# Products of 256 columns that stream their operand in exchanged runs of 16, in place of a shifted operand, in a two-layer diffusion transformer on one core

## The chip, the core and the metric

The kernel runs on one core of a Trainium2 chip. A core has a matrix engine (PE; its weight loads are listed apart, as PEld), a vector engine (DVE), a scalar engine (ACT), GpSimd (POOL), and SyncE (SP), which here only issues transfers. Matrix products read both operands from SBUF and accumulate in PSUM, which has eight banks of 512 float32 columns in each of 128 partitions. The metric is the device time of one execution in microseconds. The kernel before took 1179.38 us, the median of three runs (1178.57 to 1179.57).

A product on PE has two operands. The stationary one, `lhsT`, at most 128 columns, is put into the array by a weight load. The streamed one, `rhs`, here mostly 256 or 512 columns, then runs through the array, and each streamed column gives one column of output in PSUM. In the profile, each product is one LDWEIGHTS on PEld and one MATMUL on PE.

## The reference

One batch of 256 latent tokens and 256 context tokens, model width 1024, two layers. Layer 0 mixes by retention (4 heads, two directions) and treats both kinds of tokens; layer 1 mixes by neighbourhood attention (32 heads) and gives the latent tokens alone. After each mixer comes a gated residual, a layer norm, and an MLP of width 4096 with a squared relu:

```python
def sq_relu_mlp(h, w1, w2):
    return jnp.square(jax.nn.relu(h @ w1)) @ w2

def reference(x, c, ctx, ...):
    for i in range(DEPTH):
        ...
        x = layer_norm(DN_ALPHA * x + g1 * y, ln_g[i, 0], ln_b[i, 0])
        h = x * (1.0 + sc2) + sh2
        x = layer_norm(DN_ALPHA * x + g2 * sq_relu_mlp(h, mlp_w1[i], mlp_w2[i]), ln_g[i, 1], ln_b[i, 1])
        ...
    return x
```

All arrays are float32. The first layer's MLP is called the first MLP below, the second layer's the second MLP.

## The kernel before

**Three products for one.** Every float32 operand of a large product is split into a high part (rounded, by a cast on ACT) and a low part (the rest, by a subtraction on DVE), both of type float32r. The helper `mm3` (line 174) issues high·high, high·low and low·high into one accumulating output. In names, `hi` and `lo` are the parts of a weight, `hTh` and `hTl` those of the modulated tokens (model columns on the partitions; 8 blocks of 512 token columns, the 256 latent tokens first), `hid` those of an MLP's hidden layer, `oTh` and `oTl` those of the attention's output.

**Where 256 columns are streamed.** Most products stream 512 columns. Those with 256 are, in order of the program:

- `masked_scores` (line 1062): the retention's scores for the keys of the latent tokens, output `pS`;
- `mm1` with the latent columns and `ctx_mm1` with the context columns, for the first two blocks of the first MLP (lines 1254 and 1263), output `p1`;
- `q_mm` and part of `k_mm` (line 1445 on), the attention's queries and keys of the latent tokens, output `pn`;
- `mmo` (line 1694) with half a bank, in the attention's output projection, output `pnw`;
- `tok_part` (line 1975), the first block of the second MLP, in which the tokens are the stationary operand and the weights are streamed, output `p1t`;
- `mm1` for the other 14 blocks of the second MLP's first product, weights stationary and tokens streamed, output `p1`;
- `mm2b` (line 2094) for the last 512 columns of the second tile's output in the second MLP, which are computed in two halves of 256, output `p2`.

The profile leaves trailing digits off names, so that `p1` and `p2` are both `p` there; they are told apart by the operands (`hT…` or `hid`).

**The shift.** Every large tile starts at the same place modulo 1024 bytes, and a slice of a weight or of the tokens starts at a multiple of 128 float32 (512 bytes) from its tile's start. So the start of the streamed operand and that of the next product's stationary operand differ by a multiple of 512 bytes. The second MLP is the exception. There the token tiles' columns begin at `AT = 7 * LINE` with `LINE = 16` float32 (64 bytes): its modulated tokens are written to columns 112 to 367 of each block instead of 0 to 255, and read from there. All else in that MLP (weights, hidden layer) is unshifted. This is line 1933 with the helper `toks` in line 1937; `mm1` is told by its argument `at=AT`.

**What sets the order.** PE runs its products in the program's order. Weights come in units of 512 KB: SP fetches a unit into one of four raw tiles, ACT makes the high part and DVE the low part, into one of five buffers each. In the stretches around the change PE's own instructions are all that the program has to do in order, with `relu_sq`, the splits of weights, and norms on ACT and DVE beside it.

Of the kernel before, what the change touches and what calls it, by code (L numbers as in the profile page):

```python
# [17 lines left out]
P = 128  # L18
# [18 lines left out]
LINE = 16  # L37
# [67 lines left out]
def kernel(  # L105
# [23 lines left out]
    pe, act, dve, pool, sp = (  # L129
        InOrder(tc, getattr(nc, e), e in PIN)  # L130
        for e in ("tensor", "scalar", "vector", "gpsimd", "sync")
    )
# [23 lines left out]
    def bank(s="ps"):  # L156
        return psp.tile([P, 512], F32, tag="ps", name=nm(s))

    def slot(i, shape, dt, s):

        return arena.tile(shape, dt, tag=f"s{i}", name=nm(s))
# [4 lines left out]
    def tsl(t):  # L166
        return slice(t * P, (t + 1) * P)
# [3 lines left out]
        act.copy(out=hi_ap, in_=raw_ap)  # L171
        (eng or dve).tensor_sub(out=lo_ap, in0=raw_ap, in1=hi_ap.bitcast(F32))

    def mm3(o, a, b, start, stop):
        (ah, al), (bh, bl) = a, b
        pe.matmul(o, lhsT=ah, rhs=bh, start=start, stop=False)
        pe.matmul(o, lhsT=ah, rhs=bl, start=False, stop=False)
        pe.matmul(o, lhsT=al, rhs=bh, start=False, stop=stop)
# [76 lines left out]
    def fetch(n, in_scratch=False, at=None):  # L255

        for src, k, ncol in specs[len(units) : len(units) + max(n, 0)]:
            raw = rawp.tile([P, k, ncol], F32, tag="raw", name=nm("raw"))
            sp.dma_start(out=raw[:], in_=src.rearrange("(k p) n -> p k n", p=P))
            if in_scratch or len(units) in scratch_units:  # L260
                hi, lo = Rows([scr("hi", F32R) for _ in range(k)]), Rows([scr("lo", F32R) for _ in range(k)])
                for i in range(k):
                    act.copy(out=hi[:, i, :], in_=raw[:, i, :])
                    pending.append((lo[:, i, :], raw[:, i, :], hi[:, i, :]))
                units.append((hi, lo))
                continue
            if at is None:
                hi = hip.tile([P, k, ncol], F32R, tag="hi", name=nm("hi"))
                lo = lop.tile([P, k, ncol], F32R, tag="lo", name=nm("lo"))
            else:  # L270
                both = slot(at, [P, 2, k, ncol], F32R, "hilo")
                hi, lo = both[:, 0], both[:, 1]
            act.copy(out=hi[:], in_=raw[:])
            pending.append((lo[:], raw[:], hi[:]))
            units.append((hi, lo))

    def lows(n=100, eng=None):
        for lo, raw, hi in pending[:n]:
            (eng or dve).tensor_sub(out=lo, in0=raw, in1=hi.bitcast(F32))
        del pending[:n]  # L280

    def take(n, ahead=WB, open_=0):
        first = taken[0]
        while len(units) < min(first + max(n, ahead), len(specs)):
            fetch(1)
            lows()
        taken[0] = first + n
        assert len(units) - len(pending) >= first + n - open_
        return units[first : first + n]
# [302 lines left out]
    def mod_aff(pt, half, t, A, B, on_act=None, halves=False):  # L592

        tmp = scr("aff")
        for i in range(4):
            k = 4 * half + i
            a, b = A[:, k, t // 2 : t // 2 + 1], B[:, k, t // 2 : t // 2 + 1]
            o, x_ = tmp[:, tsl(i)], pt[:, tsl(i)]
            if halves:
                o = o.rearrange("p (b r c) -> p b r c", b=2, r=2)  # L600
                x_ = x_.rearrange("p (r b c) -> p b r c", b=2, r=2)
            if not (half if on_act is None else on_act):
                dve.tensor_scalar(out=o, in0=x_, scalar1=a, scalar2=b, op0=ALU.mult, op1=ALU.add)
            else:
                act.activation(out=o, in_=x_, func=AF.Identity, scale=a, bias=b)
        return tmp
# [299 lines left out]
    w = ws[0]  # L906
# [98 lines left out]
    for h in range(RH):  # L1005
# [9 lines left out]
        else:  # L1015
# [92 lines left out]
        for t in range(4):  # L1108
            po = bank("po")
            scs = list(range(4)) if t < 2 else [2, 3]  # L1110
            for i, sc in enumerate(scs):
                a, b = S[sc]
# [51 lines left out]
        if not last:  # L1164
            for half in range(2):
                us = take(2)
# [6 lines left out]
        else:  # L1173
# [17 lines left out]
            def turn(t):  # L1191
                return [mod_pt(xns[t], half) for half in range(2)]

            def affine(t, pts):
                return [mod_aff(pts[half], half, t, A, B) for half in range(2)]
# [51 lines left out]
    def relu_sq(ps, sl, hh, hl):  # L1247
        split(squared(ps, sl), hh, hl)
# [3 lines left out]
    LAT, ALL, CTX = slice(0, NLAT), slice(0, NT), slice(NLAT, NT)  # L1252

    def mm1(us, sl, pb, ks=range(KC), at=0):
        for i in range(2):
            for k in ks:
                wh, wl = us[k // 4]
                mm3(
                    pb[i][:, sl], (wh[:, k % 4, tsl(i)], wl[:, k % 4, tsl(i)]),
                    hs(k, at + sl.start, at + sl.stop), k == 0, k == KC - 1,  # L1260
                )

    def ctx_mm1(us, pb):
        for i in range(2):
            for k in (4, 5, 6, 7, 0, 1, 2, 3):
                pe.matmul(
                    pb[i][:, CTX], lhsT=us[k // 4][0][:, k % 4, tsl(i)], rhs=hTh[:, k, CTX],
                    start=k == 4, stop=False,
                )
        for i in range(2):  # L1270
            for k in (4, 5, 6, 7, 0, 1, 2, 3):
                wh, wl = (w[:, k % 4, tsl(i)] for w in us[k // 4])
                pe.matmul(pb[i][:, CTX], lhsT=wl, rhs=hTh[:, k, CTX], start=False, stop=False)
                pe.matmul(pb[i][:, CTX], lhsT=wh, rhs=hTl[:, k, CTX], start=False, stop=k == 3)

    G2 = None
    for hf in range(2):
# [9 lines left out]
        if hf == 0:  # L1287
            us = take(2, 2, 1)
# [5 lines left out]
            f2 = affine(2, turn(2))  # L1294
# [29 lines left out]
        for fp in range(len(hid), 8):  # L1324
            ht = hslot(fp)
            pb = [bank("p1") for _ in range(2)]
            us = take(2)
# [15 lines left out]
        for half in range(2):  # L1343
            last = hf == 1 and half == 1
            pb = [bank("p2") for _ in range(4)]
# [64 lines left out]
            p = turn(0)  # L1410
# [9 lines left out]
            p = turn(1)  # L1420
# [304 lines left out]
    f2 = [mod_aff(p2[half], half, 2, A, B, True) for half in range(2)]  # L1725
# [118 lines left out]
    n = NS - 1  # L1844
# [20 lines left out]
    us = take(2, 0)  # L1865
# [7 lines left out]
    def wo_last(t, half, cols=slice(0, 512)):  # L1873
        ps = wops[half, t, cols.start] if half else bank("pnw")
        mmo(ps, t, (4, 5, 6, 7), us[2 * half : 2 * half + 2], cols, start=half == 0)
        return ps
# [31 lines left out]
    ps = bank("pnw")  # L1908
# [21 lines left out]

    AT = 7 * LINE
    ht = slot(N_Q, [P, 4, 2, NLAT], F32R, "hid1")
    us4 = take(2, 0, 1)

    def toks(t):
        return slice(AT + t * P, AT + (t + 1) * P)

    def affine_half(pts, half, t, on_act, eng=dve):  # L1940
        aff = mod_aff(pts[half], half, t, A, B, on_act)
# [32 lines left out]

    def tok_part(ps, t, f2, a, b, ks=range(KC), start=False, stop=False):
        for k in ks:
            pe.matmul(
                ps[:, :256],
                lhsT=hs(k, toks(t).start, toks(t).stop)[a],
                rhs=us4[2 * f2 + k // 4][b][:, k % 4, :],  # L1980
                start=start and k == ks[0],
                stop=stop and k == ks[-1],
            )
# [7 lines left out]
    def turn_block(r, t, f2, ht=ht):  # L1991
        pt = bank("pt")
        for i in range(2):
            pe.transpose(pt[:, tsl(i)], r[:, tsl(i)], ident)
        src = pt[:, :256].rearrange("p (i t) -> p i t", i=2)
        hi, lo = (ht[:, 2 * f2 : 2 * f2 + 2, a, tsl(t)] for a in range(2))
        act.copy(out=hi, in_=src)
        dve.tensor_sub(out=lo, in0=src, in1=hi.bitcast(F32))
# [3 lines left out]
    ps = [wo_last(1, 1, cols) for cols in HALVES]  # L2002
# [63 lines left out]
    for f4 in range(1, 8):  # L2066
        ht = slot(HS1[f4], [P, 4, 2, NLAT], F32R, "hid1")
        for f2 in range(2):
            opening = f4 == 1 and f2 == 0
            us = take(2, 0, 2) if opening else take(2)  # L2070
            pb = [bank("p1") for _ in range(2)]
            mm1(us, LAT, pb, at=AT)
            dve.on = f4 < 3
            for i in range(2):
                relu_sq(pb[i], LAT, ht[:, 2 * f2 + i, 0, :], ht[:, 2 * f2 + i, 1, :])
                if opening:
                    fetch(1)
                    lows(1)
                if opening and i == 0:
                    turn_block(r10, 1, 0, hid[0])  # L2080
                    turn_block(r11, 1, 1, hid[0])
            if opening:
                for e in (pe, act, pool):
                    e.on = False
        hid.append(ht)
        if f4 in (1, 2):
            residual(f4 - 1, xn2[:, f4 - 1, :], gb, dve)
        dve.on = False
# [125 lines left out]
```

## Time and profile before

| | |
|---|---|
| median of the runs | 1179.38 us (1178.57 to 1179.57) |
| the profiled execution: its time | 1179.48 us |
| its span, first to last instruction | 1177.4 us |
| PE busy | 1167.3 us, 6821 products |
| PE weight loads busy | 985.6 us |
| DVE busy | 844.6 us |
| ACT busy | 480.6 us |
| POOL busy | 212.5 us |
| read from memory | 189.12 MB |

The profile is that of one execution. A span is the time from the first to the last instruction of the program; the execution's time lies 2.1 us above it. A busy time is the union of an engine's instructions, and the products on PE overlap: one that is listed with 0.28 us may begin 0.12 us after the one before. So what a product costs in a row of products is read from the starts in the timeline, not from its listed duration. The row of the granted clock counts tenths of TensorE's full speed in 40 slices of the span.

### The profile page before, as it was taken

Reading aid. Unit: us, or ns where it says so; the run is one execution under the profiler, and the core shown is the slowest. Engines: PE = TensorE matmul, PEld = TensorE weight load, DVE = VectorE, ACT = ScalarE, POOL = GpSimd, SP = SyncE. Lnnn points to the kernel's source line nnn. Section 1 sums busy time; section 2 is a strip of 40 time slices with the busy share of each in tenths; the row PEclk is TensorE's granted clock in tenths of the full one; section 3 lists DMA queues with packets and bytes.
Section 4 is the critical chain, followed back from the end, with each engine's and each line's share of the span. In section 5 each row is a group of like instructions: output and inputs, shape, how many; then the busy total and the mean of one; then the engine's idle time right before and its main releaser. Section 6 shows DMA issues by size and latency. Waiting matters only on the chain.

```text
span 1177.4 us, 17745 instructions
## 1 busy us (share of the span) xinstructions
PE 1167.3 (99%) x6821; PEld 985.6 (84%) x6821; DVE 844.6 (72%) x1349; ACT 480.6 (41%) x819; POOL 212.5 (18%) x364
## 2 busy tenths in 40 slices
PE   9999999999999999999999999999999999999997
PEld 7788888888888889888888888889888878999886
DVE  3786678787888787757767675678577589877446
ACT  3643332222323246442212333137466666665341
POOL 0103001000200241780203000223343430000001
PEclk9999999999999999999999999999999999999999
DMA  9943544544355416757566665646344334766660
GB/s 276 276 130 104 161 143 140 152 147 152 118 169 175 141 60 214 189 112 217 171 190 197 212 199 190 201 141 204 83 135 139 111 115 155 222 209 197 233 212 36
DMA packets 140115, 195.10 MB, mean 166 GB/s; under 512 B 9936, under 2 KB 81136, under 8 KB 140032
## 3 DMA queue, kind: packets, MB, share of 16 engines
q1 hardware_dynamic: 131904, 182.03, 49.4%
q0 software_dynamic: 6976, 9.39, 3.9%
q10 hardware_dynamic: 1152, 2.56, 0.7%
q8 instruction: 53, 0.87, 0.3%
q14 instruction: 30, 0.25, 0.1%
HBM read 189.12 MB, written 5.75 MB: 166 GB/s over the span
## 4 chain that ended last, share of the span: by engine, by line
PE 94%; DMA 2%; SPq 1%; ACT 1%; DVE 1%; issue 0%; POOL 0%; ACTq 0%; DVEq 0%
PE p L84 44%; PE pw L84 7%; PE pg L84 7%; PE pq L84 7%; PE pv L84 7%; PE pn L84 5%; PE pnv L84 4%; PE po L84 3%; PE ppt L84 2%; PE pnw L84 1%; PE pS L84 1%; PE pav L84 1%; PE pqk L84 1%; SPq L84 1%; PE pt L84 1%; PE p1t L84 1%
## 5 line engine op out<-in xcount | busy, mean ns | idle before, releaser
L84 ACT CAST hi<-raw 128x1024 fp32r<-128x1024 f32 (+2 forms) x228 | 231.7, 1032 | 308.9 <-PE p L84 113.4
L84 DVE TENSOR_TENSOR lo<-raw,hi 128x1024 fp32r<-128x1024 f32 (+2 forms) x228 | 273.4, 1213 | 105.5 <-ACT hi L84 105.4
L84 PE MATMUL p<-hi,hid 128*128 128x512 f32 (+1 forms) x832 | 241.8, 373 | 0.0
L84 PEld LDWEIGHTS p<-hi,hid 128*128 128x128 f32 x832 | 152.1, 188 | 27.6
L84 PE MATMUL p<-hTh,lo 128*128 128x256 f32 (+1 forms) x512 | 165.8, 326 | 0.0
L84 PE MATMUL p<-hTl,hi 128*128 128x256 f32 (+1 forms) x512 | 165.8, 326 | 0.0
L84 PE MATMUL p<-hTh,hi 128*128 128x256 f32 (+1 forms) x512 | 162.9, 328 | 0.0
L84 PE MATMUL p<-lo,hid 128*128 128x512 f32 (+1 forms) x416 | 155.2, 373 | 0.0
L84 DVE SCALAR_TENSOR_TENSOR acc<-rawa,scol,acc 128x1024 f32<-128x1024 f32 x56 | 74.5, 1342 | 66.0 <-DMA rawa<-in_ada_w_dram 66.0
L84 PEld LDWEIGHTS p<-hTh,lo 128*128 128x128 f32 x512 | 96.4, 188 | 8.8
L84 PEld LDWEIGHTS p<-hTl,hi 128*128 128x128 f32 x512 | 96.4, 188 | 8.7
L84 PEld LDWEIGHTS p<-hTh,hi 128*128 128x128 f32 x512 | 94.2, 188 | 8.7
L84 PEld LDWEIGHTS p<-lo,hid 128*128 128x128 f32 x416 | 78.4, 188 | 13.7
L84 DVE SCALAR_TENSOR_TENSOR strips<-rawa,scol,strips 128x512 f32<-128x512 f32 x112 | 78.6, 762 | 0.0
L84 ACT CAST hid<-r 128x256 fp32r<-128x256 f32 (+1 forms) x64 | 31.9, 500 | 111.2 <-DVE r L84 111.2
L84 POOL TENSOR_TENSOR rstd<-rstd,misc 128x1 f32<-128x1 f32 x28 | 19.1, 684 | 212.4 <-DVE rstd L84 211.4
L84 POOL TENSOR_TENSOR R<-R,acc 128x512 f32<-128x512 f32 x16 | 25.8, 1633 | 168.8 <-DVE acc L84 168.8
L84 ACT ACTIVATE s<-s,mn 128x512 f32<-128x512 f32 x64 | 45.5, 713 | 22.0 <-DVE mn L84 22.0
L84 PE MATMUL pw<-hi,oh 128*128 128x512 f32 x128 | 51.0, 398 | 0.0
L84 PE MATMUL pg<-hi,hTh 128*128 128x512 f32 x128 | 50.6, 395 | 0.0
L84 PE MATMUL pq<-hTh,hi 128*128 128x512 f32 x128 | 49.3, 395 | 0.8 <-ACT hTh L84 0.5
L84 PE MATMUL pw<-hi,ol 128*128 128x512 f32 x128 | 49.9, 390 | 0.0
(238 smaller groups left out, 2278.5 us busy)
## 6 DMA issues: line engine op xcount, KB each, us to landing
raw<-in_mlp_w_dram SPq DMA_DIRECT2D x128, 512.0 KB, 4.2
rawa<-in_ada_w_dram SPq DMA_DIRECT2D x80, 512.0 KB, 3.9
raw<-in_ret_w_in_dram SPq DMA_DIRECT2D x42, 512.0 KB, 3.9
raw<-in_nat_w_in_dram SPq DMA_DIRECT2D x24, 512.0 KB, 4.3
rawq<-in_ada_w_dram SPq DMA_DIRECT2D x16, 512.0 KB, 6.2
raw<-in_ret_w_o_dram SPq DMA_DIRECT2D x16, 512.0 KB, 3.4
bias<-rpb_rows POOLq DMA_DIRECT2D x32, 128.0 KB, 2.9
raw<-in_nat_w_o_dram SPq DMA_DIRECT2D x8, 512.0 KB, 3.8
```

The lines of the kernel that those rows point to most:

```text
L84: r = f(*args, **kwargs)
```

## The change

A new helper, `swapped`, takes an operand of 256 contiguous columns and returns the same columns in another order: runs of 16 (64 bytes), with each pair of runs exchanged, so 16 to 31, 0 to 15, 48 to 63, 32 to 47, and so on. It gives an access pattern of three loops (8 pairs, 2 runs with a step of minus 16, 16 columns) that starts at column 16. The streamed operand and the output are both given this order, so that each output column still lands in its place. `mm3` does this for every output of 256 columns; `ctx_mm1` and `tok_part`, which issue their products themselves, do it too. The second MLP's tokens go back to columns 0 to 255.

```diff
-    def mm3(o, a, b, start, stop):
+    def swapped(*aps):
+
+        res = []
+        for ap in aps:
+            p, (step, n) = ap.ap
+            assert step == 1 and n == 256
+            res.append(
+                bass.AP(ap.tensor, ap.offset + LINE, [list(p), [2 * LINE, n // (2 * LINE)], [-LINE, 2], [1, LINE]])
+            )
+        return res if len(aps) > 1 else res[0]
+
+    def mm3(o, a, b, start, stop, swap=True):
         (ah, al), (bh, bl) = a, b
+        if swap and o.shape[-1] == 256:
+            o, bh, bl = swapped(o, bh, bl)
         pe.matmul(o, lhsT=ah, rhs=bh, start=start, stop=False)
         pe.matmul(o, lhsT=ah, rhs=bl, start=False, stop=False)
         pe.matmul(o, lhsT=al, rhs=bh, start=False, stop=stop)
...
             for k in (4, 5, 6, 7, 0, 1, 2, 3):
                 wh, wl = (w[:, k % 4, tsl(i)] for w in us[k // 4])
-                pe.matmul(pb[i][:, CTX], lhsT=wl, rhs=hTh[:, k, CTX], start=False, stop=False)
-                pe.matmul(pb[i][:, CTX], lhsT=wh, rhs=hTl[:, k, CTX], start=False, stop=k == 3)
+                o, th, tl = swapped(pb[i][:, CTX], hTh[:, k, CTX], hTl[:, k, CTX])
+                pe.matmul(o, lhsT=wl, rhs=th, start=False, stop=False)
+                pe.matmul(o, lhsT=wh, rhs=tl, start=False, stop=k == 3)
...
-    AT = 7 * LINE
...
     def toks(t):
-        return slice(AT + t * P, AT + (t + 1) * P)
+        return slice(t * P, (t + 1) * P)
...
     def tok_part(ps, t, f2, a, b, ks=range(KC), start=False, stop=False):
         for k in ks:
+            o, w = swapped(ps[:, :256], us4[2 * f2 + k // 4][b][:, k % 4, :])
             pe.matmul(
-                ps[:, :256],
+                o,
                 lhsT=hs(k, toks(t).start, toks(t).stop)[a],
-                rhs=us4[2 * f2 + k // 4][b][:, k % 4, :],
+                rhs=w,
...
-            mm1(us, LAT, pb, at=AT)
+            mm1(us, LAT, pb)
```

No instruction changes its place on any engine. On PE the products of 256 columns change their form alone, as here in the first head's scores (`qkh` and `qkl` are the parts of queries and keys):

```order
-L84 MATMUL pS_907<-qkh_760 128x256
-L84 MATMUL pS_907<-qkl_761,qkh_760 128x256
-L84 MATMUL pS_907<-qkh_760,qkl_761 128x256
+L84 MATMUL pS_907<-qkh_760 128x8x2x16
+L84 MATMUL pS_907<-qkl_761,qkh_760 128x8x2x16
+L84 MATMUL pS_907<-qkh_760,qkl_761 128x8x2x16
```

The six rows are three products before and the same three after: 256 output columns in one loop became 8 times 2 times 16.

The built program differs in one more way, in PE's waits for itself. In 34 places PE now waits on its own semaphore for an earlier product, the nearest of them 39 instructions back; before, these waits were not there. What the other engines wait for on PE, and PE on them, is as before but for ten waits of DVE that are gone.

More of the change, by code (lines that the diff above doesn't have):

```diff
@@ L1266, in ctx_mm1 @@
                 pe.matmul(
-                    pb[i][:, CTX], lhsT=us[k // 4][0][:, k % 4, tsl(i)], rhs=hTh[:, k, CTX],
+                    swapped(pb[i][:, CTX]), lhsT=us[k // 4][0][:, k % 4, tsl(i)], rhs=swapped(hTh[:, k, CTX]),
                     start=k == 4, stop=False,
```

## The prediction

> **What bounds the kernel now.** I read the page first: the busy times, the clock, and the chain that ended last.
>
> ```profile
> span 1177.4 us, 17745 instructions
> PE 1167.3 (99%) x6821; PEld 985.6 (84%) x6821; DVE 844.6 (72%) x1349; ACT 480.6 (41%) x819; POOL 212.5 (18%) x364
> PEclk9999999999999999999999999999999999999999
> PE 94%; DMA 2%; SPq 1%; ACT 1%; DVE 1%; issue 0%; POOL 0%; ACTq 0%; DVEq 0%
> ```
>
> PE is busy for 99% of the span at full clock, and 94% of the chain is PE. The view of PE's waits has three rows for the whole program, 2.1 us in all:
>
> ```profile
> PE pq L84 <- DVE still L84: 1.2, 1, 1.2
> PE pq L84 <- ACT hTh L84: 0.5, 1, 0.5
> PE pq L84 <- DVE hTh L84: 0.4, 1, 0.4
> ```
>
> So the kernel ends when PE's products have run through, and a nanosecond per product counts unless a wait appears in its place. What a product of 256 columns costs is read from the starts in PE's timeline. First the attention's queries, unshifted, then the second MLP's first product, whose tokens are shifted by 7 runs of 64 bytes:
>
> ```profile
> 799.70 0.28 PE L84 MATMUL pn<-hTl,hi 128*128 128x256 f32 x1
> ...
> 800.90 0.28 PE L84 MATMUL pn<-hTh,lo 128*128 128x256 f32 x1
> ```
>
> ```profile
> 1011.77 0.28 PE L84 MATMUL p<-hTl,hi 128*128 128x256 f32 x1
> ...
> 1012.91 0.28 PE L84 MATMUL p<-hTh,lo 128*128 128x256 f32 x1
> ```
>
> Both pairs are ten products apart. Unshifted they take 1.20 us, 120 ns each; shifted 1.14 us, 114 each, and over a longer stretch 113.5:
>
> ```profile
> 1015.00:1070.00 55.00, 55.00 (x487) 1.00 0.65 203
> ```
>
> (55.00 us and one listed duration of 0.28, since a product counts that began before the window, over 487.) The form is the same, the engines beside it are busy in both, and the operands differ only in where they start. Nine steps of 512 columns are 2.04 us, 227 ns each, twice the faster step:
>
> ```profile
> 434.82 0.39 PE L84 MATMUL pw<-hi,ol 128*128 128x512 f32 x1
> ...
> 436.86 0.39 PE L84 MATMUL pw<-hi,ol 128*128 128x512 f32 x1
> ```
>
> So 113.4 ns is what 256 columns cost when they only stream, and some 6.6 ns more, about what 15 columns take, is paid where streamed and stationary operand start at the same place modulo 512 bytes. In rows of 512 columns the same alignment costs nothing. The weight load for the next product begins with the streaming of this one, and it too is listed longer where `pn` is unshifted than in `p`, most of which is shifted (timeline of PE and PEld, then the groups of PEld):
>
> ```profile
> 800.78 0.28 PE L84 MATMUL pn<-hTl,hi 128*128 128x256 f32 x1
> 800.78 0.19 PEld L84 LDWEIGHTS pn<-hTh,lo 128*128 128x128 f32 x1
> ```
>
> ```profile
> L84 PEld LDWEIGHTS p<-hTl,hi 128*128 128x128 f32 x512 | 96.4, 188 | 8.7
> L84 PEld LDWEIGHTS pn<-hTl,hi 128*128 128x128 f32 x144 | 27.4, 190 | 1.7
> ```
>
> My reading: the two reads meet in the same part of SBUF at the start, and the streaming loses the time of one run of 16. The 6.6 ns are a measurement, the meeting is an inference.
>
> [...]
>
> **The change part by part.** First, who is unshifted today, from the groups of PE by form:
>
> ```profile
> L84 PE MATMUL p<-hTh,lo 128*128 128x256 f32 x288 | 78.7, 278 | 0.0
> L84 PE MATMUL pn<-hTh,lo 128*128 128x256 f32 x96 | 27.2, 284 | 0.0
> L84 PE MATMUL p<-hi,hid 128*128 128x256 f32 x128 | 25.2, 282 | 0.0
> L84 PE MATMUL p<-lo,hid 128*128 128x256 f32 x64 | 18.1, 283 | 0.0
> L84 PE MATMUL p1t<-lo,hTh 128*128 128x256 f32 x32 | 4.8, 280 | 0.0
> L84 PE MATMUL pS<-qkl,qkh 128*128 128x256 f32 x16 | 4.5, 283 | 0.0
> L84 PE MATMUL pnw<-lo,oTh 128*128 128x256 f32 x12 | 3.4, 283 | 0.0
> ```
>
> Each kind has three products, so `p<-hT` counts 3 x 288 = 864. Of these the second MLP has 14 blocks x 2 x 8 x 3 = 672, shifted, and the first MLP 192, unshifted. Further unshifted: `pn` 3 x 96 = 288, the hidden layer's 128 + 64 = 192, `pS` 48, `pnw` 48 (36 as listed, 12 more whose weights lie in another buffer). Together 768. `p1t` has 96, and there the shift is on the stationary side.
>
> Step 1, the exchange for the 768. At the start the streamed operand now asks for run 1 while the weight load asks for run 0, as with a shift by an odd number of runs. If that does what the shift does, each goes from 120 to 113.4: 768 x 6.6 ns = 5.1 us. Not all of it is there to be had. The first product after a stretch of 512 columns costs 0.11 already, and after transposes it takes four steps to settle even in the shifted stretch:
>
> ```profile
> 437.09 0.28 PE L84 MATMUL p<-hTh,hi 128*128 128x256 f32 x1
> 437.20 0.28 PE L84 MATMUL p<-hTl,hi 128*128 128x256 f32 x1
> 1004.49 0.28 PE L84 MATMUL p<-hTl,hi 128*128 128x256 f32 x1
> ...
> 1004.97 0.28 PE L84 MATMUL p<-hTh,lo 128*128 128x256 f32 x1
> ```
>
> (four steps in 0.48 us, 26 ns over the streaming rate). For such starts, an estimate of 15 in all, I take off 0.4 us: 4.7.
>
> Step 2, `p1t`. Its starts:
>
> ```profile
> 991.17 0.62 PE L84 MATMUL p1t<-hi,hTh 128*128 128x256 f32 x4
> 991.62 0.62 PE L84 MATMUL p1t<-lo,hTh 128*128 128x256 f32 x4
> ...
> 997.31 0.63 PE L84 MATMUL p1t<-hi,hTh 128*128 128x256 f32 x4
> 997.78 0.63 PE L84 MATMUL p1t<-lo,hTh 128*128 128x256 f32 x4
> ```
>
> Four products take 0.45 us at first (113 ns each), after a stall 0.47 (117.5). With the stationary tokens shifted, the same shift works once and half works later. If the exchange works always, the later 70 or so save 4 ns each: 0.3 us.
>
> Step 3, the second MLP's 672. They lose the shift and get the exchange: from 113.5 to 113.4, nothing, if the exchange is as good. If it did nothing they would fall back to 120: 672 x 6.5 = 4.4 us lost.
>
> Step 4, the pattern itself. The streamed operand and the output jump 16 times per product. On the read side the nearest rows are the small products of the modulation, whose streamed columns are 16 bytes apart in the forms of 16 and 8 columns and adjacent in those of 64 and 32:
>
> ```profile
> L84 PE MATMUL pada<-red,cst 128*32 128x64 f32 x4 | 0.6, 231 | 0.0
> L84 PE MATMUL pada<-red,cst 128*32 128x32 f32 x4 | 0.5, 206 | 0.0
> L84 PE MATMUL pada<-red,cst 128*32 128x16 f32 x32 | 1.0, 196 | 0.0
> L84 PE MATMUL pada<-red,cst 128*32 128x8 f32 x16 | 0.5, 186 | 0.0
> ```
>
> The adjacent ones give 25 ns for 32 columns; carried down, 16 columns should take 194 and 8 take 188. They take 196 and 186, so a jump at every column costs nothing to be seen, at most 2 ns in 16. For 16 jumps in each of 864 + 288 + 192 + 96 + 48 + 48 = 1536 products that is 0 to 3 us. I take 0, since the two rows differ from the line in opposite directions. On the write side no product of the trace writes PSUM with jumps. From below the price is 0; the far bound is that jumping writes bring the stream down to the slowest rate in these rows, 25 ns for 32 columns or 0.78 each: 256 x 0.78 = 200 ns in place of 113, 1536 x 87 ns = 133 us. The read side is the nearer row, so I take 0 and keep the rest as a rival.
>
> Step 5, the 34 waits of PE for itself. The nearest asks for a product 39 instructions back. These started at least a microsecond earlier (the ten steps above take 1.14) and are listed with 0.28 us: nothing. That cover is gone only where PE is not the bound.
>
> Step 6, the unshifted write of the tokens by ACT and DVE: same instructions and sizes, nothing.
>
> What is late next: where PE speeds up, the weights' parts must keep pace. In the second MLP they already do at 113.5 ns, so they do elsewhere at that rate.
>
> Sum, against the profiled execution: 1179.5 (span 1177.4 and 2.1 around it) minus 4.7 minus 0.3 gives 1174.5. That execution lies 0.1 above the median of 1179.38, so I forecast **1174.5 us** for the median, 0.4% less.
>
> **The rivals.**
>
> Half an exchange. Run by run, 1, 0, 3, 2 is ahead of the plain order at even places and behind it at odd ones. If the weight load meets the stream at the wrong places, the steady step is `p1t`'s later 117.5 ns everywhere. For: the shift of 7 on the streamed side gives 113.5, on the stationary side, where it counts the other way, 117.5, so it is not only odd or even that decides. Against: `p1t` also ran at 113 before its stall. Price: 768 x 2.5 = 1.9 saved, 672 x 4.0 = 2.7 lost: 1180.3.
>
> No exchange. The order within a pair does not matter to SBUF, only the distance of the two starts. Then the 768 stay at 120, and the 672 fall back to it, 4.4 us: 1183.9. For: only distances have been varied in the trace. Against: the loss is one run's length, and the exchange moves the first runs apart.
>
> Jumps cost. Each of the 16 jumps takes one column's time, 0.44 ns (113.4 / 256), in reading or writing: 7.1 ns per product. With the meeting avoided this is 1536 x 7.1 = 10.9 lost and 5.0 saved: 1185.4. It decides from 5.0 us / 1536 = 3.3 ns per product, half a column per jump. Against it are the rows of 16 and 8 columns; for it, that no row shows a jumping write. [...] The far end of this rival is the 133 us above, 1307 less what is saved.
>
> **How the numbers follow.** The exchange works as the shift does: 0.53. Half: 0.13. No exchange: 0.14. Jumps at about a column each: 0.13. Jumps at much more: 0.07. The likeliest's own range is 1173.2 (nothing lost at the starts, so 5.4 saved, and 0.8 of the 1.0 us by which the runs of before differ) to 1176.5 (a jump price of 1.3 ns per product, 2.0 us). The range over the cases is 1173.2 to 1186.0: it takes in the first four cases and leaves out the 0.07 above it, part of the fourth, and a little below. A measurement of this kernel tells about 0.2%, 2.4 us, from no change. Faster by more: the first case, 0.53, less a little where part of it is lost, with as much from a mild jump price: 0.53. Within: the half exchange, 0.13. Slower: the last three, 0.34.
>
> **What would show it.** Right: in the timeline the steps of `pn`, `pS`, `pnw` and of both `p` are 113 to 114 ns, and the listed durations 276 to 278 in place of 283; the second MLP's span from 1004 to 1081 us keeps its length. Half: 117 to 118 everywhere. No exchange: 120 everywhere, the second MLP longer by 4.4 us. Jumps: all steps above 120, the same excess in every group. Wrong in another way: new rows in PE's waits, or a step of 512 columns that is no longer 227.

## The result, and the profile after

The changed kernel takes 1183.38 us, the median of eight runs (1183.06 to 1187.39), against 1179.57 for the kernel before, also of eight (1178.48 to 1181.57): a ratio of 1.0033, with a 95% interval of 1.0022 to 1.0044. It is slower by 3.8 us where 4.9 us less was forecast. The time lies inside the range and on the wrong side.

The profiled execution took 1183.26 us. Its page, the rows that were shown of before:

```profile
span 1181.2 us, 17743 instructions
PE 1171.2 (99%) x6821; PEld 990.0 (84%) x6821; DVE 846.5 (72%) x1349; ACT 482.7 (41%) x819; POOL 212.8 (18%) x364
PEclk9999999999999999999999999999999999999999
PE 97%; DMA 1%; DVE 1%; ACT 1%; issue 0%; POOL 0%; DVEq 0%; ACTq 0%
```

The granted clock is 0.999 in the mean (0.998 before), PE is as close to always busy as before (99% of the span), and the chain is PE's to 97%. No wait took the time (PE's waits come to 2.2 us, 2.1 before): the products themselves became slower. How much, and between which ends, is read from PE's timeline at the first product of 256 columns and at the last product of the program. Before:

```profile
77.11 0.28 PE L84 MATMUL pS<-qkh 128*128 128x256 f32 x1
...
1169.49 0.28 PE L84 MATMUL p<-hi,hid 128*128 128x256 f32 x1
```

After:

```profile
76.21 0.28 PE L84 MATMUL pS<-qkh 128*128 128x256 f32 x1
...
1173.31 0.28 PE L84 MATMUL p<-hi,hid 128*128 128x256 f32 x1
```

From the one to the other it was 1092.38 us and is 1097.10, so 4.7 us are lost. Ahead of the first, where nothing was changed, this execution happened to be 0.9 us quicker, which gives the 3.8 us between the two profiled times.

Where the 4.7 us lie, the steps tell. The second MLP's first product in the timeline of after, two rows ten products apart:

```profile
1039.71 0.28 PE L84 MATMUL p<-hTl,hi 128*128 128x256 f32 x1
...
1040.91 0.28 PE L84 MATMUL p<-hTh,lo 128*128 128x256 f32 x1
```

That is 120 ns each, where it was 114. In the view by windows (window, its length, PE's busy time with the count of products, clock, DMA share, GB/s) the stretch that held 487 products before now holds 461:

```profile
1015.00:1070.00 55.00, 55.00 (x461) 1.00 0.64 193
```

The attention's queries, which were to gain, stayed at 120 ns, but in turns of a shorter and a longer step:

```profile
799.47 0.28 PE L84 MATMUL pn<-hTl,hi 128*128 128x256 f32 x1
799.58 0.28 PE L84 MATMUL pn<-hTh,lo 128*128 128x256 f32 x1
799.71 0.28 PE L84 MATMUL pn<-hTh,hi 128*128 128x256 f32 x1
...
800.91 0.28 PE L84 MATMUL pn<-hTl,hi 128*128 128x256 f32 x1
```

Twelve steps take 1.44 us, 120 each; in the records' nanoseconds the turns are 117 and 123, or 118 and 122. Over all steps of 256 columns that follow one another, from start to start in ns (the count of steps after the group's name):

| group | before | after |
|---|---|---|
| `pS` (47) | 119.2 | 119.9 |
| first MLP, tokens streamed (190) | 119.8 | 120.0 |
| `pn` (281) | 119.8 | 120.0 |
| `pnw` (47) | 119.8 | 120.0 |
| `p1t` (some 90) | 117.0 | 120.0 |
| second MLP, tokens streamed (670) | 113.4 | 120.0 |
| hidden layer (191) | 119.4 | 119.9 |

670 x 6.6 ns = 4.4 us and 90 x 3.0 = 0.3 us make the 4.7. The steps of 512 columns are as before, 227.4 against 227.3 ns in the mean of some 3757. So the exchange gave nothing to any group, and it did not replace the shift. The experiments ask why.

### The profile page after: what moved, and what is told of

Same layout as the page of the kernel before. It is cut to its first block, busy times and chain, and to the rows that moved or that the text cites. A ratio compares the mean times of both kernels' runs of the same rounds, so it can differ in the third digit from the quotient of the medians.

```text
span 1181.2 us, 17743 instructions
## 1 busy us (share of the span) xinstructions
PE 1171.2 (99%) x6821; PEld 990.0 (84%) x6821; DVE 846.5 (72%) x1349; ACT 482.7 (41%) x819; POOL 212.8 (18%) x364
## 4 chain that ended last, share of the span: by engine, by line
PE 97%; DMA 1%; DVE 1%; ACT 1%; issue 0%; POOL 0%; DVEq 0%; ACTq 0%
PE p L84 44%; PE pq L84 8%; PE pv L84 7%; PE pw L84 7%; PE pg L84 7%; PE pn L84 5%; PE pnv L84 4%; PE po L84 3%; PE ppt L84 2%; PE pnw L84 1%; PE pS L84 1%; PE pav L84 1%; PE pada L84 1%; PE pqk L84 1%; PE pt L84 1%; PE p1t L84 1%
## 5 line engine op out<-in xcount | busy, mean ns | idle before, releaser
L84 PE MATMUL pg<-hi,hTl 128*128 128x512 f32 x128 | 49.9, 390 | 0.0
```

The lines of the kernel that those rows point to most:

```text
L84: r = f(*args, **kwargs)
```

## Experiments

All step times below are such differences of starts on PE, in ns. A kernel's time is of one execution where nothing else is said, so the argument goes by the steps within an execution and not by times that differ by 2 or 3 us. "Distance" is the start of the streamed operand minus that of the stationary one, in runs of 16 columns (64 bytes). For an exchanged operand it goes by the first of its columns, as for a plain one, and not by the run that is read first.

### One side at a time

The first kernel exchanges the streamed operand alone, the second the output alone; both keep the second MLP's shift of 7. In both, the output's columns land in other places. The third exchanges both and keeps the shift.

```diff
-            o, bh, bl = swapped(o, bh, bl)
+            bh, bl = swapped(bh, bl)        # streamed operand alone
+            o = swapped(o)                  # output alone
...
+    AT = 7 * LINE
-        return slice(t * P, (t + 1) * P)
+        return slice(AT + t * P, AT + (t + 1) * P)
```

> The exchange is made for the streamed operand alone; outputs are written in plain order, so their columns stand in exchanged places (part of what is computed is changed), and the second MLP's tokens are shifted by 7 runs as before. Three theories. Meeting: jumps are free, the stream and the weight load still meet. Then the unshifted products stay at a mean of 120 ns, in turns of 118 and 122 as in the changed kernel, and the second MLP's first product moves to another value than 113.4, by its new distance. Read jumps: each of the 16 jumps in reading costs about a cycle, 6.6 ns per product; then every group has a mean of 120, shifted or not. Write jumps: reading is free and the exchange avoids the meeting; then every group is at 113.4, and the kernel takes about 1174.5 us.

> The exchange is made for the output alone (its columns stand in exchanged places, so part of what is computed is changed); streamed operands are read in plain order, the second MLP's tokens shifted by 7 runs as before. Meeting, or read jumps: writing with jumps is free, so all is as in the kernel before: 113.4 ns in the second MLP's first product, 120 in the unshifted groups, 1179.4 us. Write jumps: the second MLP's first product goes to about 120, the unshifted groups to 120 to 127, the kernel to 1184 us or more.

> The changed kernel with the second MLP's tokens shifted by 7 runs again; all is computed. If a jump has a price of its own, in reading or in writing (read jumps, write jumps), the second MLP's first product stays near 120 ns and the kernel near 1183.4 us. Meeting: the shift moves the starts apart again and the step becomes another one, between 113.4 and 120 ns and not the same turns of 118 and 122; at 113.4 the kernel takes 1179 us.

The kernel before took 1178.63 us beside them.

| kernel | time, us | second MLP | `p1t` | other groups |
|---|---|---|---|---|
| streamed operand alone, shift 7 | 1186.06 | 120.0 | 117.9 | 119.9 to 120.0 |
| output alone, shift 7 | 1180.98 | 117.5 | 115.7 | 119.3 to 119.9 |
| both, shift 7 | 1183.13 | 120.0 | 117.9 | 119.9 to 120.1 |

The exchange in reading alone takes the shift's gain away, in whichever order is written (120.0 both times, 113.4 in the kernel before). That is 6.6 ns for 16 jumps; the cycle in which expectations count here is this over 16, an estimate of 0.41 ns, and no run shows a cycle's length. (The 1186.06 holds a late start besides: its first `pS` begins at 79.0 us, against 76.2 in the change; from there to the last product it takes 1097.3 us against 1097.1.) The exchange in writing leaves the unshifted groups where they were (119.3 to 119.9, before 119.2 to 119.8). Its 117.5 in the second MLP needs a closer look, in PE's timeline of that kernel:

```profile
1007.19 0.28 PE L84 MATMUL p<-hTl,hi 128*128 128x256 f32 x1
...
1008.32 0.28 PE L84 MATMUL p<-hTh,lo 128*128 128x256 f32 x1
...
1008.78 0.60 PE L84 MATMUL pt<-cst,r 128*128 128x128 f32 x4
1009.14 0.36 PE L84 MATMUL p<-hTh,hi 128*128 128x256 f32 x1
...
1011.81 0.28 PE L84 MATMUL p<-hTl,hi 128*128 128x256 f32 x1
...
1012.99 0.28 PE L84 MATMUL p<-hTh,lo 128*128 128x256 f32 x1
```

Ten products of one and the same form take 1.13 us before the transposes (`pt`) and 1.18 us after them, and it stays at 118 to the end of the stretch. If writing had a price, the first ten would pay it too. So there are two steady steps, 113 and 118, and after an interruption the products can go on at the other.

### The loops without the exchange

The three-loop pattern in plain order, with the shift of 7:

```diff
-                bass.AP(ap.tensor, ap.offset + LINE, [list(p), [2 * LINE, n // (2 * LINE)], [-LINE, 2], [1, LINE]])
+                bass.AP(ap.tensor, ap.offset, [list(p), [2 * LINE, n // (2 * LINE)], [LINE, 2], [1, LINE]])
```

> The pattern of three loops is kept, with a step of plus 16 in place of minus 16 and no offset, so the order of columns is the plain one and nothing jumps; second MLP shifted by 7 runs; all is computed. All three theories: as before, 113.4 ns shifted and 120 unshifted, 1179.4 us. If the loops themselves had a price, the shifted products would be slower than 113.4; at one cycle for each of 16 runs they would be at 120 and the kernel at 1184 us.

It took 1179.62 us. But in the built program runs in plain order are one loop again, so this was a second execution of the kernel before and tells nothing of the loops. It does tell that the step of 118 is not the exchange's: in the second MLP some 45 products from 1004.5 us on ran at 117.8 and the rest at 113, with plain order on both sides.

### Longer runs

The change with runs of 64 columns, and of 32, in place of 16 (no shift):

```diff
-ap.offset + LINE, [list(p), [2 * LINE, n // (2 * LINE)], [-LINE, 2], [1, LINE]]
+ap.offset + R, [list(p), [2 * R, n // (2 * R)], [-R, 2], [1, R]]      # R = 4 * LINE, then 2 * LINE
```

> The changed kernel with runs of 64 columns exchanged in place of 16 (4 runs per product, not 16), second MLP not shifted; all is computed. Price per jump: 4 jumps x 0.41 = 1.7 ns, so 115 ns if the new distance of 4 runs avoids the meeting and 121 to 122 if not; 1175.5 us or 1184.5. Meeting alone: nothing says what a distance of 4 runs gives; 113.4 or 117.8 if it is good, 120 if not, with no excess for jumps. A price for each run of 16 columns whether exchanged or not (none of the theories) would leave 120.

> As the run with 64, with runs of 32 columns (8 per product). Price per jump: 8 x 0.41 = 3.3 ns, 116.7 ns if the distance of 2 runs avoids the meeting, 123 if not. Meeting alone: the same step as with some plain distance, 113.4, 117.8 or 120.

1182.64 and 1183.09 us: all groups at 119.2 to 120.0 with runs of 64, and at 118.7 to 119.9 with runs of 32; the second MLP 120.0 and 119.9. The step does not follow the number of jumps: 16, 8 and 4 of them all leave it at 118.7 to 120.0, so a price for each jump is not what holds it there. More than that these two kernels cannot tell. With runs of 64 columns the exchange starts four runs further on, and at a distance of 4 plain order stands at 119.8 as well (the table of distances below), so no gain was to be had.

### 512 columns exchanged

The kernel before, with the exchange in `mm3`'s products of 512 columns instead (all is computed):

```diff
+        if o.shape[-1] == 512:
+            o, bh, bl = swapped(o), swapped(bh), swapped(bl)
```

> The kernel before, with the exchange made in mm3 for the products of 512 columns alone, streamed operand and output; those of 256 stay plain and shifted as before; all is computed. [...] Meeting alone: 227 ns as before, 1179 us.

1208.62 us. In PE's timeline of it, thirteen steps take 3.08 us, 237 ns each:

```profile
299.87 0.40 PE L84 MATMUL po<-vh,sl 128*128 128x512 f32 x1
...
302.95 0.40 PE L84 MATMUL po<-vh,sh 128*128 128x512 f32 x1
```

The mean over 3758 steps is 235.4, 8.0 above plain order; 3758 x 8.0 = 30 us, which accounts for the loss of 29. At 512 columns plain order at distance 0 takes 227.4 ns, twice the shifted 256 columns' 113.4 but for 0.6, and so has next to no loss that an exchange could have removed; here it shows a price of its own.

### The distance, in rows of their own

To take distance and order apart, rows of 36 products (24 of 512 columns) stand behind the finished kernel, with nothing beside them. All of the reference is computed; the time of 1332.87 us is that of the kernel and the rows.

```diff
+    def row(name, n, d, turn, count, width=P, read=True, write=True):
+        ps = bank(name)
+        for j in range(count):
+            o = ps[:width, :n]
+            s = fh[:, 512 * (j % 4) + LINE * d : 512 * (j % 4) + LINE * d + n]
+            if turn and write:
+                o = exchanged(o)
+            if turn and read:
+                s = exchanged(s)
+            w = fl[:, 512 * (j % 8) : 512 * (j % 8) + width]
+            pe.matmul(o, lhsT=w, rhs=s, start=j == 0, stop=j == count - 1)
```

> The kernel before with rows of products added behind its last one, whose results are not used: for every distance d from 0 to 7 runs of 16 between the starts of the streamed and the stationary operand, 36 products of 256 columns in plain order (ya to yh) and in exchanged order (za to zh), and 24 of 512 in plain order (va to vh; exchanged wa, wh for d 0 and 7); 36 with a stationary operand of 32 columns in place of 128, plain and exchanged (spa, sxa, sph, sxh); and 36 with the exchange in reading alone (rxa, rxh) or in writing alone (oxa, oxh). Only differences between rows of this run count. Meeting: a load of a quarter of the columns is over early, so exchanged and plain products with it are equal, both near 113.4 ns or both up to one run's time above; oxa is as ya and oxh as yh; plain rows depend on d with 113.4 at d 7 and 120 at d 0, exchanged rows depend on d too, and their best d is below 120. Price of jumps in reading: sxa and sxh are 6.6 ns above spa and sph, and every exchanged row za to zh is at 120 or above. Price of jumps in writing: oxh is 6.6 ns above yh.

PE's timeline of it. `ya` to `yh` are plain at distances 0 to 7, `za` to `zh` exchanged in reading and writing; `spa` and `sxa` are plain and exchanged at distance 0 with 32 stationary columns in place of 128, which is called the short load below, and `sph` and `sxh` the same at distance 7. `rxa` and `rxh` are exchanged in reading alone, `oxa` and `oxh` in writing alone, at distances 0 and 7 with the full load. `va` to `vh` have 512 plain columns, `wa` and `wh` 512 exchanged ones at distances 0 and 7. A row's step is the difference to the next row's start, divided by 36 or 24:

```profile
1172.24 4.48 PE L84 MATMUL ya<-hTh,hTl 128*128 128x256 f32 x36
1176.57 4.41 PE L84 MATMUL yb<-hTh,hTl 128*128 128x256 f32 x36
...
1185.08 4.25 PE L84 MATMUL yd<-hTh,hTl 128*128 128x256 f32 x36
1189.17 4.46 PE L84 MATMUL ye<-hTh,hTl 128*128 128x256 f32 x36
...
1201.99 4.25 PE L84 MATMUL yh<-hTh,hTl 128*128 128x256 f32 x36
1206.08 4.48 PE L84 MATMUL za<-hTh,hTl 128*128 128x256 f32 x36
1210.40 4.41 PE L84 MATMUL zb<-hTh,hTl 128*128 128x256 f32 x36
...
1218.88 4.48 PE L84 MATMUL zd<-hTh,hTl 128*128 128x256 f32 x36
1223.19 4.48 PE L84 MATMUL ze<-hTh,hTl 128*128 128x256 f32 x36
...
1240.31 4.25 PE L84 MATMUL spa<-hTh,hTl 128*32 128x256 f32 x36
1244.40 4.40 PE L84 MATMUL sxa<-hTh,hTl 128*32 128x256 f32 x36
1248.64 4.25 PE L84 MATMUL sph<-hTh,hTl 128*32 128x256 f32 x36
...
1269.91 4.40 PE L84 MATMUL oxh<-hTh,hTl 128*128 128x256 f32 x36
1274.15 5.65 PE L84 MATMUL va<-hTh,hTl 128*128 128x512 f32 x24
...
1290.73 5.76 PE L84 MATMUL vd<-hTh,hTl 128*128 128x512 f32 x24
1296.33 5.62 PE L84 MATMUL ve<-hTh,hTl 128*128 128x512 f32 x24
1301.79 5.67 PE L84 MATMUL vf<-hTh,hTl 128*128 128x512 f32 x24
```

`ya` takes 4.33 us, 120 ns a product, and `yd` 4.09, or 114; `sxa` takes 4.24, 118, and `spa` 4.09. Without each row's first six steps the means are:

| distance | 0 | 1 | 2 | 3 | 4 | 5 | 6 | 7 |
|---|---|---|---|---|---|---|---|---|
| 256 plain | 120.0 | 117.8 | 118.6 | 113.3 | 119.8 | 117.8 | 118.6 | 113.3 |
| 256 exchanged | 119.9 | 117.7 | 117.8 | 120.0 | 119.9 | 117.7 | 117.9 | 120.0 |
| 512 plain | 227.4 | 228.9 | 232.8 | 233.4 | 226.7 | 228.9 | 232.8 | 233.4 |

Three things follow. Both lines of 256 columns repeat after four runs, 256 bytes. An exchanged row depends on the distance as well, but in another way: none of the eight is below 117.7, at distances 3 and 7 it is the worst where plain order is the best, and at 0, where the change put every product, it is at 120 like plain order. And 512 columns want the opposite of 256: distance 3 costs them 6 ns (`vd` takes 5.60 us, `ve` 5.46).

The kernels agree with the table. In the kernel with both sides exchanged and a shift of 7, the second MLP has a distance of 7 and ran at 120.0, and `p1t`, whose distance of -7 is 1 modulo 4, at 117.9.

With the short weight load (32 columns) the rows at distances 0 and 7 agree: plain 113.3 both times, exchanged 117.7 both times. So at distance 0 the load has a part in the plain step of 120.0. And with a load that is far shorter (in the profile of before, loads of 32 columns are listed with 109 ns and those of 128 mostly with 188) the exchange still costs 4.4 ns.

Exchanged in reading alone, `rxa` and `rxh` stand at 119.9 and 120.0, as with both sides. In writing alone, `oxa` at distance 0 is at 119.9 like plain order, but `oxh` at distance 7 is at 117.8 (4.24 us) where `yh` had 113.3. That can be a price of writing or the second steady step; the next rows ask which. With 512 columns, `wa` takes 236.5 against 227.4 plain at distance 0, and `wh` 237.9 against 233.4 at distance 7.

### The parts of the price

A second set of rows takes the exchange's two sides and the length of the runs apart. `sp` to `sd` have the short load and distance 0: plain, exchanged in reading, in writing, in both, then in both with runs of 32, 64 and 128. The others have the full load and distance 7: `ya` and `yc` to `yf` are plain, `oa` and `ob` exchanged in writing, `za` in both. `yb` (256 columns) and `va` (512) are plain at distance 0. The last two, `vb` and `vc`, have 512 columns, exchanged and plain, with the short load at distance 0.

```diff
+    row("sp", 256, 0, 36, 32)
+    row("sr", 256, 0, 36, 32, read=16)
+    row("so", 256, 0, 36, 32, write=16)
+    row("sa", 256, 0, 36, 32, read=16, write=16)
+    row("sb", 256, 0, 36, 32, read=32, write=32)
...
+    row("yc", 256, 7, 36)
+    row("oa", 256, 7, 36, write=16)
+    row("yd", 256, 7, 36)
+    row("za", 256, 7, 36, read=16, write=16)
+    row("ye", 256, 7, 36)
+    row("ob", 256, 7, 36, write=16)
+    row("yf", 256, 7, 36)
+    row("vb", 512, 0, 24, 32, read=16, write=16)
+    row("vc", 512, 0, 24, 32)
```

> Rows of products behind the kernel before, as in e9_rows; results not used. With a load of 32 columns, so that no meeting disturbs: plain (sp), exchanged in reading alone (sr), in writing alone (so), in both (sa), and in both with runs of 32, 64 and 128 columns (sb, sc, sd). e9_rows gave 113.3 plain and 117.7 exchanged there. Price of jumps in reading, 4.3 ns for 16: sr 117.7, so 113.3, sb 115.5, sc 114.4, sd 113.9. Price in writing: so 117.7, sr 113.3. Second question: oxh (writing alone, distance 7) stood at 117.8 where yh stood at 113.3, but plain rows at distance 7 know both steps. Rows at distance 7, plain (ya, yc, yd, ye, yf) and exchanged in writing (oa, ob), follow different rows here. Two modes that a row takes up when it begins: some plain rows are at 117.8 too, and an exchanged one that follows a row at 113.3 without a stall keeps 113.3. Price of jumps in writing: all plain rows 113.3, both oa and ob 117.8. Last, 512 columns with a load of 32, exchanged (vb) and plain (vc): price in reading, 8.7 ns above, 235.4 against 226.7.

PE's timeline of it:

```profile
1170.56 4.40 PE L84 MATMUL sp<-hTh,hTl 128*32 128x256 f32 x36
1174.80 4.40 PE L84 MATMUL sr<-hTh,hTl 128*32 128x256 f32 x36
1179.04 4.25 PE L84 MATMUL so<-hTh,hTl 128*32 128x256 f32 x36
1183.13 4.40 PE L84 MATMUL sa<-hTh,hTl 128*32 128x256 f32 x36
1187.37 4.25 PE L84 MATMUL sb<-hTh,hTl 128*32 128x256 f32 x36
1191.46 4.26 PE L84 MATMUL sc<-hTh,hTl 128*32 128x256 f32 x36
...
1213.65 4.26 PE L84 MATMUL yc<-hTh,hTl 128*128 128x256 f32 x36
1217.75 4.24 PE L84 MATMUL oa<-hTh,hTl 128*128 128x256 f32 x36
1221.83 4.24 PE L84 MATMUL yd<-hTh,hTl 128*128 128x256 f32 x36
1225.91 4.49 PE L84 MATMUL za<-hTh,hTl 128*128 128x256 f32 x36
1230.23 4.40 PE L84 MATMUL ye<-hTh,hTl 128*128 128x256 f32 x36
1234.47 4.40 PE L84 MATMUL ob<-hTh,hTl 128*128 128x256 f32 x36
1238.71 4.40 PE L84 MATMUL yf<-hTh,hTl 128*128 128x256 f32 x36
1242.95 5.77 PE L84 MATMUL vb<-hTh,hTl 128*32 128x512 f32 x24
1248.56 5.71 PE L84 MATMUL vc<-hTh,hTl 128*32 128x512 f32 x24
```

Writing in exchanged runs is free: `so` takes 4.09 us for 36, and `oa` 4.08 between plain rows of 4.10 and 4.08. `ob` takes 4.24, but so do the plain rows before and behind it, `ye` and `yf`. Each of the two goes on at the step of the plain row ahead of it, 113.3 or 117.8, so the 117.8 of `oxh` needs no price of writing. Reading in exchanged runs of 16 takes 4.24 (`sr`, and `sa` with writing too). Runs of 32 (`sb`) are free again with this load (4.09 us for 36), with 8 jumps in place of 16, and so are 64 and 128 (113.3). So the price is that of reading neighbouring runs of 64 bytes in exchanged order, and not so much for each jump.

`sp` is the odd one: plain, and 4.24 us, where the same row had 113.3 in the first set. It is the second steady step again. Its rhythm differs from that of the exchanged rows (117, 118, 119 in `sp`; 115, 119, 120 in turn in `sr`, `sa`, `sxa`, `zb`), and rows of this form that read in plain order show both steps, while the four that read in exchanged runs of 16 (`sxa`, `sxh`, `sr`, `sa`) never show the faster.

The 512 columns with the short load came out otherwise than expected: exchanged `vb` 233.4 ns and plain `vc` 231.5, where 235.4 and 226.7 were expected. `vc` has three steps of 226 and 227 near its start and then goes in turns of 229 to 234, slower than `va` of the same set with the full load (226.7). So the 8.0 ns of 512 columns are shown for the full load; with the short load the two differ by 1.9, and why that plain row is slow stays open.

### Tiles moved apart

If the distance is what counts, whole tiles can be moved instead. This kernel was measured before the rows above, so its expectation does not know them. It is the kernel before without its shift, with two unused tiles of 64 bytes, one ahead of the weights' tiles and one ahead of the others.

```diff
+    gap0 = ec(tc.tile_pool(name="gap0", bufs=1)).tile([P, LINE], F32, tag="gap0", name="gap0")
     rawp = ec(tc.tile_pool(name="rawp", bufs=4))
...
+    gap1 = ec(tc.tile_pool(name="gap1", bufs=1)).tile([P, LINE], F32, tag="gap1", name="gap1")
     arena = ec(tc.tile_pool(name="arena", bufs=1))
...
-    AT = 7 * LINE
+    AT = 0
```

> The kernel before without any exchange and without the shift of 7 runs; instead an unused tile of 64 bytes stands ahead of the weights' buffers and another ahead of the arena that holds hidden layers and attention outputs, so that nearly every streamed operand starts one run of 64 bytes ahead of the stationary one, modulo 512 bytes, which is what a shift of 7 makes of it. All is computed. If the distance of the two starts is what costs, whatever makes it: pn, pnw, the first MLP and the hidden layer's 256 columns go from 120 to 113.4 (or to 117.8, the other step that the shifted products show after some stalls), the second MLP stays at 113.4, pS and part of pnw stay at 120: 720 x 6.4 = 4.6 us less than before, 1174.5 to 1175.5. If the distance of the starts is not it (7 runs of 64 bytes as such, or the tokens' columns): the second MLP goes back to 120 and the kernel to 1184 us.

1197.29 us, the median of four runs, against 1179.88 of seven beside them: a ratio of 1.0144 (1.0123 to 1.0164), where 4.6 us less were expected. The first MLP's 256 columns fell to 115.1, `pn` to 114.3, the hidden layer to 113.7; the second MLP ran at the other steady step, 117.8. But the 512 columns went from 227.3 to 232.4. In PE's timeline nine of them take 2.10 us, where it was 2.04:

```profile
434.54 0.40 PE L84 MATMUL pw<-hi,ol 128*128 128x512 f32 x1
...
436.64 0.39 PE L84 MATMUL pw<-hi,ol 128*128 128x512 f32 x1
```

3759 x 5.0 ns = 19 us lost and 670 x 4.4 = 2.9 lost in the second MLP, against some 4 gained, make about the 17.4 us between the medians. As the rows of 512 columns show, the distance that is good for 256 is bad for 512, and both use the same tiles.

### Forecasts from the rows

Two kernels test the table. The change with a shift of 1 should run the second MLP at the exchanged row's 117.7; the kernel before with a shift of 3 should run it like a shift of 7, at one of the two plain steps.

```diff
+    AT = 1 * LINE      # in the change
...
-    AT = 7 * LINE
+    AT = 3 * LINE      # in the kernel before
```

> The changed kernel with the second MLP's tokens shifted by 1 run of 16; all is computed. The rows give the exchanged order 120.0 ns at distances 0 and 3 modulo 4 and 117.7 at 1 and 2. If that holds in the kernel: the second MLP's first product falls from 120.0 to 117.7, 672 x 2.3 = 1.5 us, 1181.8 us; all else as in the changed kernel. If the loss in the changed kernel is the jumps' alone, the shift changes nothing: 120.0 and 1183.3.

> The kernel before with a shift of 3 runs in place of 7; all is computed. If the distance counts modulo 4 runs (256 bytes), as in the rows: 113.4 ns in the second MLP's first product (or 117.8, the other step of that distance), and the kernel at 1179 us (or 1181.5). If 7 is special: another step, 120 at worst, 1183.5 us.

The first: second MLP 117.8 in the same rhythm of 115, 118, 120, all other groups 119.9 to 120.0, and 1183.36 us. That is 1.5 more than the steps give, because in this execution PE waited for a weight's low part at a place that was not changed. In PE's timeline (in brackets the idle time before, and for whom):

```profile
768.91 0.61 PE L84 MATMUL p<-hi,hid 128*128 128x512 f32 x2
770.97 0.50 PE L84 MATMUL p<-lo,hid 128*128 128x512 f32 x1 [1.44 <-DVE lo L84]
```

Without that wait it is 1181.9. The second: 117.8 throughout the second MLP, and 1181.23 us, the same stretch by windows holding 469 products:

```profile
1015.00:1070.00 55.00, 55.00 (x469) 1.00 0.65 201
```

So a shift of 3 can run at the second step, as a shift of 7 did in part. The same may account for much of the spread of the kernel before (1178.48 to 1181.57 over its eight runs), since 670 x 4.4 ns = 2.9 us lie between the two steps. It is not shown, because only one of these eight has a profile, and that one ran at 113.

## Why the prediction was wrong, point by point

**What bounds the kernel: right.** Nothing but PE's steps moved, and 4.7 us of them came out as 4.7 us between the first and the last product concerned.

**The reading of the meeting: right in part.** That the step depends on where the two operands start is shown by the rows of one form at eight distances, and that the weight load has a part in it by the short load at distance 0 (113.3, or 117.8 in `sp`, against 120.0). The trace was read as modulo 512 bytes; the rows repeat after 256 (plain, 120.0 at distance 0 and 119.8 at 4, 113.3 at 3 and at 7). At distances 1 and 3 plain order gives 113.3 or 117.8. The prediction did not see that these are two steps of one form: the 117.5 of `p1t`, from which it made the rival "half an exchange", fits the second of them, at distance -7, which is 1 modulo 4.

**Step 1, the failed one.** "If that does what the shift does, each goes from 120 to 113.4." It does not. The rows at distance 0 split the 6.6 ns. From plain with the short load (`spa`, 113.3) to exchanged with the short load (`sxa`, 117.7) it is 4.4 ns, which go with reading neighbouring runs in exchanged order; no row that reads so is below 117.7, whatever its distance. From there to exchanged with the full load (`za`, 119.9) it is another 2.2 ns, which go with the weight load and which the exchange does not avoid at distance 0. Step 1 rested on the first 16 columns alone: the exchange puts them at an odd distance, and that was taken for the whole product. The forecast had 4.7 us gained here, and the runs showed none.

**Step 2** fell with it: `p1t` went from 117.0 to 120.0, 0.3 us lost in place of 0.3 gained.

**Step 3** was put at nothing under the same condition. Its other branch, 4.4 us lost if the exchange did nothing, is what came.

**Step 4, the pattern's zero: right for writing, wrong for reading.** `so` and `oa` show jumping writes at 113.3, while reading so costs 4.4 ns (`sxa` 117.7, `spa` 113.3). For reading, the rows of 16 and 8 columns were the wrong neighbours: their columns lie apart but in rising order, and no row of before had runs that step back.

**Steps 5 and 6: right.** The 34 waits of PE for itself show in no row of PE's waits after, which are four, 2.2 us in all, for DVE and DMA; the chain is PE's own time to 97%.

**The rivals.** "No exchange" was nearest: 120 ns everywhere and 4.4 us in the second MLP, 1183.9 against 1183.38. Its reason does not hold, since the order within a pair does matter (117.7 against 113.3 with the short load, and the turns of 117 and 123). "Jumps cost" named a price on the read side that exists, but it is not a price for each jump (runs of 32 cost nothing with the short load, 113.3), and in the changed kernel the groups' means did not go above 120.0.

**What stays open.** Why exchanged runs of 64 bytes cost 4.4 ns and runs of 128 bytes nothing, whether this is the same loss as that of the second plain step with its equal mean, and what decides which of the two plain steps a row takes up. No run leaves the weight load out altogether, so that a meeting of the exchanged reads with even the short load is not excluded.

## What to carry to other kernels

A trick that works through where two operands start is to be tried as rows of one form at several distances before it is built on; eight rows of 36 products cost 34 us of one run and would have turned this forecast round. The distance has to be chosen for the products that carry the time, and here the many products of 512 columns want the one that is bad for 256 (distance 0: 227.4 against 233.4 ns at distance 3; of 256 columns, 120.0 against 113.3). Where a step of the sum says "does what the other does", the first thing to ask is which part of the other's gain the new form cannot have.

## What the runs showed of the hardware

- The step of a product of 256 float32r columns with a full weight load repeats, over distances of 0 to 7 runs of 64 bytes between the two starts, every 256 bytes: 120.0, 117.8 (in `p1t` also 113), 118.6, 113.3 (or 117.8) ns for 0, 1, 2 and 3 runs. Of 512 columns it is 227, 229, 233, 233.
- Plain products of one form at a distance of 7 runs, or with the short load, have two steady steps, 113.3 and 117.8 ns. In the second MLP of the kernels with a shift of 7 they kept one from the sixth step on through stretches of 46 and 622 steps, and changed it only between the two.
- Writing PSUM in exchanged runs of 64 bytes is free (`so`, `oa`: 113.3 ns). Reading SBUF so costs 4.4 ns in 256 columns with the short load (117.7 against 113.3), and the exchange on both sides 8.0 ns in 512 with the full load at distance 0 (235.4 against 227.4; there the two sides were not run apart). With 256 columns and the short load, runs of 128 bytes and more cost nothing (113.3).
